# A 1-D max pool on one core: every load first, outputs kept on chip, stores queued behind the last load in longer runs

## The chip, the core and the metric

The kernel runs on one core of a Trainium2 chip. The metric is the device time in microseconds of one execution.

## The reference

The input is 32 x 256 rows of 4096 fp32 values. Each row is cut into 256 windows of 16 values, and the output is the maximum of each window.

```
x: (32, 256, 4096) float32, output_size = 256
for i in range(output_size):
    start = int(i * length / output_size)
    end = int((i + 1) * length / output_size)
    result[:, :, i] = np.max(x[:, :, start:end], axis=-1)
```

So 8192 rows of 16 KB come in (134.2 MB), and 8192 rows of 1 KB go out (8.4 MB). There is one comparison for each value. The work is moving bytes.

## The kernel before

Rows are dealt out in 7 groups of 9 rows for each of the 128 partitions, with one more row per partition at the end. A ring of nine 16 KB slots in SBUF, the memory on the chip, takes three loads of three rows. Each load reads a contiguous run of 48 KB per partition. VectorE reduces row by row into an output tile of the group. Two groups are stored while loads still run; five are "held" and stored behind the loads. Towards the end the loads get smaller (three, two, two, one, one rows, then quarters of a row), so that VectorE has little left to do when the last bytes arrive.

```python
    RING = 9
    G = 9
    N_GROUPS = 7
    LOAD = 3
    LATE = [3, 2, 2, 1, 1]
    HELD = 4
    PIECES = 4
    # ... ring, 6 output tiles, last_out; row = (g * 128 + p) * 9 + r
    for g in range(N_GROUPS):
        o = outs[g % len(outs)]
        sizes = LATE if g == N_GROUPS - 1 else [LOAD] * (G // LOAD)
        r = 0
        for n in sizes:
            at = n_read % RING
            nc.sync.dma_start(out=ring[:, at : at + n], in_=xg[g][:, r : r + n])
            for i in range(n):
                nc.vector.reduce_max(
                    out=o[:, (r + i) * O : (r + i + 1) * O],
                    in_=ring[:, at + i],
                    axis=mybir.AxisListType.X,
                )
            n_read += n
            r += n
        if g < N_GROUPS - 1 - HELD:
            nc.scalar.dma_start(out=og[g], in_=o)     # groups 0 and 1: among the loads
        else:
            held.append((og[g], o))
    # ... the last row, in PIECES pieces
    for dst, src in held:
        nc.sync.dma_start(out=dst, in_=src)           # five stores behind the loads
    nc.scalar.dma_start(out=ol, in_=last_out)
```

Of the kernel before, what the change touches and what calls it, by code (L numbers as in the profile page):

```python
# [1 line left out]

# [4 lines left out]


@with_exitstack
def kernel(  # L10
    ctx: ExitStack,
    tc: tile.TileContext,
    x: bass.AP,
    output_size: bass.AP,
    out: bass.AP,
):



    nc = tc.nc  # L20
    P = nc.NUM_PARTITIONS
    fp32 = mybir.dt.float32

    B, C, L = x.shape
    O = int(output_size)
    assert L % O == 0, (L, O)
    W = L // O
    xf = x.flatten_outer_dims()
    of = out.flatten_outer_dims()
    rows = xf.shape[0]  # L30
    assert rows == 64 * P

    RING = 9
    G = 9
    N_GROUPS = 7
    LOAD = 3
    LATE = [3, 2, 2, 1, 1]
    HELD = 4
    PIECES = 4

    pool = ctx.enter_context(tc.tile_pool(name="pool", bufs=1))
    ring = pool.tile([P, RING, O, W], fp32, tag="ring", name="ring")
    outs = [
        pool.tile([P, G * O], fp32, tag=f"out{i}", name=f"out{i}")
        for i in range(N_GROUPS - 1)
    ]
    last_out = pool.tile([P, O], fp32, tag="lastout", name="lastout")

    main = N_GROUPS * G * P
    xg = xf[0:main].rearrange("(g p r) (o w) -> g p r o w", p=P, r=G, w=W)  # L50
    og = of[0:main].rearrange("(g p r) m -> g p (r m)", p=P, r=G)
    xl = xf[main:rows].rearrange("p (o w) -> p o w", w=W)
    ol = of[main:rows]

    n_read = 0
    held = []
    for g in range(N_GROUPS):
        o = outs[g % len(outs)]
        sizes = LATE if g == N_GROUPS - 1 else [LOAD] * (G // LOAD)
        r = 0  # L60
        for n in sizes:
            at = n_read % RING
            nc.sync.dma_start(out=ring[:, at : at + n], in_=xg[g][:, r : r + n])
            for i in range(n):
                nc.vector.reduce_max(  # L65
                    out=o[:, (r + i) * O : (r + i + 1) * O],
                    in_=ring[:, at + i],
                    axis=mybir.AxisListType.X,
                )
            n_read += n  # L70
            r += n
        if g < N_GROUPS - 1 - HELD:
            nc.scalar.dma_start(out=og[g], in_=o)
        else:
            held.append((og[g], o))

    at = n_read % RING
    oc = O // PIECES
    for c in range(PIECES):
        cut = slice(c * oc, (c + 1) * oc)  # L80
        nc.sync.dma_start(out=ring[:, at, cut], in_=xl[:, cut])
        nc.vector.reduce_max(  # L82
            out=last_out[:, cut], in_=ring[:, at, cut], axis=mybir.AxisListType.X
        )

    for dst, src in held:
        nc.sync.dma_start(out=dst, in_=src)
    nc.scalar.dma_start(out=ol, in_=last_out)


# [1 line left out]
_INS = ['x', 'output_size']  # L92
_OUTS = [((32, 256, 256), 'float32')]

_NUMBERS = {'output_size': 256}


# [26 lines left out]
```

## Time and profile before

| | before |
|---|---|
| time, median of 3 runs | 336.75 us (336.65 to 336.76) |
| span in the profile | 334.8 us |
| bytes moved | 142.6 MB, mean 426 GB/s |
| VectorE busy | 278.8 us, 83% |
| first data packet starts / last ends | 1.74 / 333.63 us |

Lines of the page of the kernel before: the busy engines, the row of DMA share by slice (40 slices, in tenths, 9 is 90% or more), packets, the queue of instruction fetches (packets, MB, share of 16 engines), the chain that ended last, and the costliest group (busy us, mean ns of one, idle time before it).

```profile
span 334.8 us, 174 instructions
...
DVE 278.8 (83%) x67; POOL 0.2 (0%) x4
...
DMA  9899999999998999899998999989999999999997
...
DMA packets 5041, 142.62 MB, mean 426 GB/s; under 512 B 560, under 2 KB 688, under 8 KB 1200
...
q14 instruction: 1, 0.01, 0.0%
...
DMA 61%; DVE 34%; issue 2%; DVEq 0%
...
L65 DVE TENSOR_REDUCE out<-ring 128x256 f32<-128x4096 f32 x63 | 274.3, 4412 | 50.0 <-DMA ring<-in_x_dram 50.0
```

A packet is what one of the 16 DMA engines moves at a time; here it is one contiguous run, so a run of 48 KB is one packet. The DMA row is full from end to end; that is the limit. The chain (61% DMA, 34% DVE) must not be read as a division of the blame. It passes through reductions because a load has to wait for a ring slot. While it waits there, one other load is being moved and another is queued, so the engines that move data are not idle.

The windows view shows this in numbers. Its columns are the window, its length, the busy time of VectorE with its number of instructions, the same for GpSimd, the clock, the DMA share, and GB/s. A packet is counted where it starts and with its whole time, so a short window can come out a little above 1.00.

```profile
20.00:60.00 40.00, 37.01 (x9) 0.00 (x0) 1.00 1.00 433
60.00:80.00 20.00, 14.36 (x4) 0.00 (x0) 1.00 1.00 420
...
314.00:326.00 12.00, 12.00 (x5) 0.00 (x0) 1.00 1.02 424
...
331.00:335.00 4.00, 0.00 (x0) 0.00 (x0) 1.00 0.43 173
```

The rate is 433 GB/s while only loads run. The Trainium skill, "DMA: Bandwidth & Descriptors", section "Where 436 GB/s comes from", gives a ceiling of 435 GB/s for the 16 ports; this trace agrees. The same section adds that between HBM, the memory that holds input and output, and SBUF a lower limit of about 358 GB/s binds; here, with one core at work, it does not, and the measurement decides. At 433 GB/s the 142.6 MB take 329.4 us of the 334.8. Little more than 5 us could be gained by any rearrangement, and start and end need part of that.

Next, lines of the timeline of the kernel before (start us, duration us, engine, line, operation, output<-input, count, idle time before and its releaser): the reductions on both sides of the first store, and the tail.

```profile
61.38 13.07 DVE L65 TENSOR_REDUCE out<-ring 128x256 f32<-128x4096 f32 x3 [1.46 <-DMA ring<-in_x_dram]
78.72 13.07 DVE L65 TENSOR_REDUCE out<-ring 128x256 f32<-128x4096 f32 x3 [4.27 <-DMA ring<-in_x_dram]
...
285.24 39.03 DVE L65 TENSOR_REDUCE out<-ring 128x256 f32<-128x4096 f32 x9 [1.53 <-DMA ring<-in_x_dram]
...
294.88 29.75 SPq L87 DMA_DIRECT2D out_dram<-out  x5
324.19 4.59 DVE L82 TENSOR_REDUCE lastout<-ring 128x64 f32<-128x1024 f32 x4
328.81 0.34 ACTq L88 DMA_DIRECT2D out_dram<-lastout  x1
```

Reductions of one load take 13.07 us and normally start 14.53 us apart. After the store among the loads the step is 78.72 - 61.38 = 17.34 us: 2.8 us for the store. VectorE ends at 328.8, close to the end of the span.

### The profile page before, as it was taken

The numbers are of one execution on the slowest core, as the hardware profiler recorded it, in microseconds if no ns is written. First come the engines' busy times: TensorE is split into PE (matmuls) and PEld (weight loads), VectorE is DVE, ScalarE is ACT, GpSimd is POOL, SyncE is SP. The second block draws the span as 40 slices with busy tenths as digits, with TensorE's granted clock in tenths as the row PEclk, the third lists the DMA queues.
The fourth block names the chain that finished last, engine by engine and source line by source line (L and its number), as shares of the span: only waits on it lengthen the run. The fifth ranks groups of instructions, "written<-read, shape, count | busy, mean of one in ns | idle before, by whom it ended". The sixth has DMA issues, their size and how long they took to land.

```text
span 334.8 us, 174 instructions
## 1 busy us (share of the span) xinstructions
DVE 278.8 (83%) x67; POOL 0.2 (0%) x4
## 2 busy tenths in 40 slices
DVE  0088989885988959798988989898898988999992
POOL 0000000000000000000000000000000000000000
DMA  9899999999998999899998999989999999999997
GB/s 370 382 470 446 399 470 393 461 386 439 435 464 382 429 464 464 382 470 423 423 470 376 470 452 393 470 382 464 452 393 470 399 446 431 435 416 411 411 433 315
DMA packets 5041, 142.62 MB, mean 426 GB/s; under 512 B 560, under 2 KB 688, under 8 KB 1200
## 3 DMA queue, kind: packets, MB, share of 16 engines
q1 hardware_dynamic: 4608, 140.12, 97.4%
q10 hardware_dynamic: 432, 2.49, 1.8%
q14 instruction: 1, 0.01, 0.0%
HBM read 134.22 MB, written 8.39 MB: 426 GB/s over the span
## 4 chain that ended last, share of the span: by engine, by line
DMA 61%; DVE 34%; issue 2%; DVEq 0%
DMA ring<-in_x_dram 61%; DVE out L65 33%; DVE lastout L82 1%; DVEq L119 0%; DVEq L65 0%
## 5 line engine op out<-in xcount | busy, mean ns | idle before, releaser
L65 DVE TENSOR_REDUCE out<-ring 128x256 f32<-128x4096 f32 x63 | 274.3, 4412 | 50.0 <-DMA ring<-in_x_dram 50.0
L82 DVE TENSOR_REDUCE lastout<-ring 128x64 f32<-128x1024 f32 x4 | 4.6, 1208 | 0.0
L105 POOL MEMSET const-bfloat16-1.0<- 128x1 bf16 x1 | 0.1, 102 | 0.0
L105 POOL MEMSET const-uint8-127<- 128x1 uint8 x1 | 0.1, 102 | 0.0
L105 POOL MEMSET const-float32-0.0<- 128x1 f32 x1 | 0.1, 99 | 0.2 <-issue 0.2
L105 POOL MEMSET const-float32-1.0<- 128x1 f32 x1 | 0.1, 99 | 0.0
## 6 DMA issues: line engine op xcount, KB each, us to landing
ring<-in_x_dram SPq DMA_DIRECT2D x19, 6144.0 KB, 30.5
ring<-in_x_dram SPq DMA_DIRECT2D x2, 4096.0 KB, 30.0
out_dram<-out SPq DMA_DIRECT2D x5, 1152.0 KB, 14.8
ring<-in_x_dram SPq DMA_DIRECT2D x2, 2048.0 KB, 30.9
out_dram<-out ACTq DMA_DIRECT2D x2, 1152.0 KB, 21.5
ring<-in_x_dram SPq DMA_DIRECT2D x4, 512.0 KB, 27.8
out_dram<-lastout ACTq DMA_DIRECT2D x1, 128.0 KB, 5.2
```

Of the source, the lines that this page charges most:

```text
L65: nc.vector.reduce_max(out=o[:, (r + i) * O : (r + i + 1) * O], in_=ring[:, at + i], axis=mybir.AxisListType.X,)
L82: nc.vector.reduce_max(out=last_out[:, cut], in_=ring[:, at, cut], axis=mybir.AxisListType.X)
L105: nc = _bacc.Bacc("TRN2", target_bir_lowering=False, num_devices=1)
```

## The change

The change puts all loads first, in 48 KB runs to the end; keeps all outputs in SBUF; and queues all stores behind the last load, in runs of 21 KB for each partition instead of 9 KB. The groups become three of 21 rows. The small late loads go, and so does the tile for the last row: its result lands in a ring slot that is free by then.

```diff
-    G = 9
-    N_GROUPS = 7
+    G = 21
+    N_GROUPS = 3
     LOAD = 3
-    LATE = [3, 2, 2, 1, 1]
-    HELD = 4
-    PIECES = 4
+    CUT = 15
     ...
     for g in range(N_GROUPS):
-        o = outs[g % len(outs)]
-        sizes = LATE if g == N_GROUPS - 1 else [LOAD] * (G // LOAD)
-        ...
-        if g < N_GROUPS - 1 - HELD:
-            nc.scalar.dma_start(out=og[g], in_=o)
-        else:
-            held.append((og[g], o))
+        for r in range(0, G, LOAD):
+            at = n_read % RING
+            nc.sync.dma_start(
+                out=ring[:, at : at + LOAD], in_=xg[g][:, r : r + LOAD]
+            )
+            for i in range(LOAD):
+                pooled(outs[g][:, (r + i) * O : (r + i + 1) * O], ring[:, at + i])
+            n_read += LOAD
     ...
+    spare = ring[:, (at + LOAD) % RING].rearrange("p o w -> p (o w)")[:, 0:O]
+    nc.sync.dma_start(out=ring[:, at], in_=xl)
+    pooled(spare, ring[:, at])
+    for g in range(N_GROUPS - 1):
+        nc.sync.dma_start(out=og[g], in_=outs[g])
+    for a, b in ((0, CUT), (CUT, G)):
+        nc.sync.dma_start(
+            out=og[N_GROUPS - 1][:, a * O : b * O],
+            in_=outs[N_GROUPS - 1][:, a * O : b * O],
+        )
-    nc.scalar.dma_start(out=ol, in_=last_out)
+    nc.scalar.dma_start(out=ol, in_=spare)
```

More of the change, by code (lines that the diff above doesn't have):

```diff
@@ L44 @@
         pool.tile([P, G * O], fp32, tag=f"out{i}", name=f"out{i}")
-        for i in range(N_GROUPS - 1)
+        for i in range(N_GROUPS)
     ]
-    last_out = pool.tile([P, O], fp32, tag="lastout", name="lastout")
     main = N_GROUPS * G * P
@@ L53, with pooled @@
     ol = of[main:rows]
+    def pooled(dst, src):
+        nc.vector.reduce_max(out=dst, in_=src, axis=mybir.AxisListType.X)
     n_read = 0
-    held = []
     for g in range(N_GROUPS):
-        o = outs[g % len(outs)]
-        sizes = LATE if g == N_GROUPS - 1 else [LOAD] * (G // LOAD)
-        r = 0
-        for n in sizes:
+        for r in range(0, G, LOAD):
             at = n_read % RING
-            nc.sync.dma_start(out=ring[:, at : at + n], in_=xg[g][:, r : r + n])
-            for i in range(n):
-                nc.vector.reduce_max(
-                    out=o[:, (r + i) * O : (r + i + 1) * O],
-                    in_=ring[:, at + i],
-                    axis=mybir.AxisListType.X,
-                )
-            n_read += n
-            r += n
-        if g < N_GROUPS - 1 - HELD:
-            nc.scalar.dma_start(out=og[g], in_=o)
-        else:
-            held.append((og[g], o))
-    at = n_read % RING
-    oc = O // PIECES
-    for c in range(PIECES):
-        cut = slice(c * oc, (c + 1) * oc)
-        nc.sync.dma_start(out=ring[:, at, cut], in_=xl[:, cut])
-        nc.vector.reduce_max(
-            out=last_out[:, cut], in_=ring[:, at, cut], axis=mybir.AxisListType.X
-        )
-    for dst, src in held:
-        nc.sync.dma_start(out=dst, in_=src)
-    nc.scalar.dma_start(out=ol, in_=last_out)
+            nc.sync.dma_start(
[4 more added lines that the diff above has]
+            n_read += LOAD
+    at = n_read % RING
+    spare = ring[:, (at + LOAD) % RING].rearrange("p o w -> p (o w)")[:, 0:O]
[7 more added lines that the diff above has]
+            in_=outs[N_GROUPS - 1][:, a * O : b * O],
+        )
+    nc.scalar.dma_start(out=ol, in_=spare)
 _INS = ['x', 'output_size']
```

## The prediction

> **What bounds the kernel now: bytes through the 16 DMA engines.** The windows view gives a DMA share of 1.00 and 433 GB/s from 20 to 60 us and about 416 to 429 GB/s in the tail from 285 to 330 us. The Trainium skill, "DMA: Bandwidth & Descriptors", section "Where 436 GB/s comes from", states a ceiling of 435 GB/s; this trace agrees. All 142.6 MB at 433 GB/s would take 329.4 us of the 334.8 us span. VectorE is 83% busy; in the timeline it takes 13.07 us for a load that arrives every 14.53 us, so it waits for DMA (50.0 us in the wait view). The chain's 34% DVE misleads: a load waits there for a ring slot while two other loads keep the engines full.
>
> **Where the 334.8 us go** (packet records of the trace). First packet at 1.74 us. Then packet time, summed and divided by 16 engines: about 330.4 us at median packet times, plus 1.2 us of packets slower than the median (start-up packets; some at 60 to 75 us, where the first store mixes with loads). The engines run out between 332.5 and 333.6 us; the end follows 1.2 us later.
>
> **Bytes do not change:** 134.2 MB in, 8.4 MB out.
>
> **What it does to packets.** Medians: 48 KB 1815 ns, 32 KB 1216, 16 KB 615, 9 KB 347, 4 KB 161, 1 KB 46; a fit is 0.0366 ns per byte plus 9 to 15 ns per packet. Estimates from it: 21 KB 799, 15 KB 573, 6 KB 235 ns. New sum: 2688 x 1815 + 128 x (615 + 2 x 799 + 573 + 235 + 46) = 5.27 ms, over 16 = 329.5 us: 1.0 us less. About half comes from the loads (4 KB pieces and the 16 and 32 KB loads), half from the 21 KB stores. Not mixing stores 1 and 2 into the load stream saves an estimated 0.2 to 0.3 us more.
>
> **What it moves.** Two stores, about 2.7 us each, leave the middle (17.3 and 17.0 us between starts of reductions become 14.5), and come back as writes at the end: off the load path, but not off the DMA engines. So the last 48 KB load lands earlier, near 308 us, the last 16 KB load near 313, and VectorE ends near 326 instead of 328.8. The stores, 19 us, run from 313 to about 332. Each is queued before its turn (the fourth near 321, its turn near 330). The small last store, issued near 326, gets in between. Pure writes already run at full rate: 347 ns a packet from 320 to 333 us. So VectorE's longer last reduction (about 4.4 us against pieces of 1.2) is hidden.
>
> **Critical path:** DMA engines throughout, so only the saved packet time counts: 1.3 us of 336.75. Time 335.4 us; 8 in 10: 334.7 to 336.3. Faster by over 2%: 0.005; within 2%: 0.98; slower: 0.015.
>
> **Right if the profile shows:** DMA share 1.00 from 3 to 331 us; reductions every 14.5 us without the two longer gaps; 21 KB packets near 800 ns; VectorE ending 6 us before the last packet; first packet and end gap unchanged.
>
> **Wrong if:** the new row pitch (336 instead of 144 KB between partitions) makes 48 KB packets slower than 1815 ns; a 19 us burst of writes slows below 27 bytes per ns per engine; or a store's issue is held by a semaphore (eight DMAs in rotation) so that the engines run dry before the end.

## The result, and the profile after

| | before | after |
|---|---|---|
| time, median of 6 runs each | 336.70 us (336.60 to 336.76) | 336.06 us (335.97 to 336.26) |
| span in the profile | 334.8 us | 334.3 us |
| data packets for each DMA engine | 280 | 216 |
| data packet time, summed, over 16 engines | 331.58 us | 330.64 us |
| last data packet ends | 333.63 us | 332.96 us |

The ratio is 0.9982, with a 95% interval from 0.9969 to 0.9995. Ratios are the mean time of one kernel's fast runs over that of the other's of the same rounds, so not quite the ratio of the medians. The change is a gain of about 0.6 us, 0.2%.

The same lines of the page of the changed kernel, with all its DMA queues:

```profile
span 334.3 us, 157 instructions
...
DVE 278.8 (83%) x64; POOL 0.2 (0%) x4
...
DMA  9899999999999999999999999999999999999997
...
DMA packets 3889, 142.62 MB, mean 427 GB/s; under 512 B 432, under 2 KB 560, under 8 KB 688
...
q1 hardware_dynamic: 3744, 142.48, 98.9%
q10 hardware_dynamic: 144, 0.13, 0.1%
q14 instruction: 1, 0.01, 0.0%
...
DMA 68%; DVE 26%; DVEq 2%; SPq 0%; issue 0%
...
L53 DVE TENSOR_REDUCE out<-ring 128x256 f32<-128x4096 f32 x63 | 274.5, 4412 | 47.6 <-DMA ring<-in_x_dram 47.6
```

VectorE is busy for the same 278.8 us, and the same 142.62 MB move in fewer packets. The chain now says 68% and 26%. That shift of 7 to 8 points went with a change of 0.2% in time: another reason not to read the chain as a division of the blame.

The same windows of the changed kernel:

```profile
20.00:60.00 40.00, 37.10 (x9) 0.00 (x0) 1.00 1.00 433
60.00:80.00 20.00, 17.08 (x5) 0.00 (x0) 1.00 1.00 433
...
314.00:326.00 12.00, 12.00 (x3) 0.00 (x0) 1.00 1.00 429
...
331.00:335.00 4.00, 0.00 (x0) 0.00 (x0) 1.00 0.25 98
```

The stretch from 60 to 80 us, which held the first store, is now pure loading at 433 GB/s. At the other end, 314 to 326 us are now stores alone, at 429 GB/s: a long burst of writes runs at nearly the rate of the loads. The DMA engines stop earlier in the last window: 98 instead of 173 GB/s.

The timeline of the changed kernel, around the place where the first store was, and the tail:

```profile
62.01 13.07 DVE L53 TENSOR_REDUCE out<-ring 128x256 f32<-128x4096 f32 x3 [1.45 <-DMA ring<-in_x_dram]
76.55 13.07 DVE L53 TENSOR_REDUCE out<-ring 128x256 f32<-128x4096 f32 x3 [1.47 <-DMA ring<-in_x_dram]
...
284.82 0.90 SPq L72 DMA_DIRECT2D out_dram<-out  x2
293.09 29.40 SPq L74 DMA_DIRECT2D out_dram<-out  x2
...
322.05 4.41 DVE L53 TENSOR_REDUCE ring<-ring 128x256 f32<-128x4096 f32 x1
326.49 0.38 ACTq L78 DMA_DIRECT2D out_dram<-ring  x1
```

The 17.34 us step is gone (76.55 - 62.01 = 14.54). The stores are issued at 284.8, 285.3, 293.1 and 322.2 us (the line with "29.40" covers the last two), while loads keep the engines busy until about 313. VectorE ends at 326.46, 6.5 us before the end of the last packet. Nearly all that the prediction named as signs is there, and the time lies in its range; the DMA share is 0.96 from 3 to 20 us and 0.98 from 326 to 331 us in the windows view, and not 1.00. The size is off: 0.64 us gained instead of 1.3.

The packet records of the trace show the durations themselves (median ns; estimates from the prediction in the last column):

```
packet     before   after   predicted
48 KB      1815     1818    1815
21 KB      -        799     799
15 KB      -        573     573
9 KB       347      -       -
6 KB       -        234     235
1 KB       46       46      46
```

The estimates for single packets hold within 1 ns except the 48 KB one. It is 3 ns longer, and 168 of them an engine make 0.5 us of recorded time. The new row pitch (the distance in memory between the rows of two partitions) is not the reason. In the changed kernel the median is 1815 ns in the first five loads and 1818 to 1820 ns from the seventh on, and it is the same at the old pitch in the second run below, which has no store among the loads either. In the kernel before, the packets stay at 1815 ns until the eleventh load, past both of its stores among the loads, and rise only then; in a run below with seven stores among the loads they stay there until the fourteenth. Landings are 14.50 us apart with the short packets and 14.53 us with the long ones. Against the kernel before this costs the changed one about 0.2 us (up to 4 ns for each of 8 packets an engine, in loads 6 to 12). Why a store among the loads has this effect is open.

The question for the experiments is what the records are worth in time, and which part of the change brings the 0.6 us.

### The profile page after: what moved, and what is told of

Same layout as the page of the kernel before. It is cut to its first block, busy times and chain, and to the rows that moved or that the text cites. A ratio compares the mean times of both kernels' runs of the same rounds, so it can differ in the third digit from the quotient of the medians.

```text
span 334.3 us, 157 instructions
## 1 busy us (share of the span) xinstructions
DVE 278.8 (83%) x64; POOL 0.2 (0%) x4
## 2 busy tenths in 40 slices
DMA packets 3889, 142.62 MB, mean 427 GB/s; under 512 B 432, under 2 KB 560, under 8 KB 688
## 4 chain that ended last, share of the span: by engine, by line
DMA 68%; DVE 26%; DVEq 2%; SPq 0%; issue 0%
DMA ring<-in_x_dram 68%; DVE out L53 25%; DVEq L109 2%; DVE ring L53 1%; SPq L59 0%
## 5 line engine op out<-in xcount | busy, mean ns | idle before, releaser
L53 DVE TENSOR_REDUCE ring<-ring 128x256 f32<-128x4096 f32 x1 | 4.4, 4410 | 0.0
```

The costliest lines, as they stand in the source:

```text
L53: nc.vector.reduce_max(out=dst, in_=src, axis=mybir.AxisListType.X)
```

## Experiments

Theory A: the 16 DMA engines are the limit from end to end, and a packet costs less than its record says, because successive packets overlap a little (the records of one instant add up to 16.02 to 16.4 busy engines out of 16). Rival B: the gain comes from taking the stores out of the middle. Rival C: recorded packet time counts in full. Later a theory F joins: the slowest of the 16 engines sets the end.

### One part of the change at a time

The first four runs were made on one chip, beside each other. The first keeps the stores of before and takes the new load sizes.

```diff
-    LATE = [3, 2, 2, 1, 1]
-    PIECES = 4
+    LATE = [3, 3, 3]
+    PIECES = 1
```

> Only the load sizes change (all 48 KB runs to the end, last load in one 16 KB piece); the seven 9 KB-run stores stay as before. Theory A (the 16 DMA engines are the limit, but successive packets overlap by some 6 ns, so a packet's recorded time does not count in full): 40 fewer load packets per engine, about 0.25 us less, 336.45. Rival C (recorded packet time counts in full): 0.49 us less, 336.2. Rival B (the gain comes from getting stores out of the middle): unchanged, 336.7.

Measured: 336.90 us (336.77 to 337.03), ratio 1.0005 (0.9992 to 1.0017), against 336.72 for before. A and C expected a gain that did not come; the interval holds B's "unchanged", but the trace shows another reason than B's. The timeline of this run's tail shows why:

```profile
314.97 13.07 DVE L65 TENSOR_REDUCE out<-ring 128x256 f32<-128x4096 f32 x3 [1.83 <-DMA ring<-in_x_dram]
327.96 4.41 DVE L82 TENSOR_REDUCE lastout<-ring 128x256 f32<-128x4096 f32 x1
...
332.40 0.34 ACTq L88 DMA_DIRECT2D out_dram<-lastout  x1
```

With the two stores still among the loads, the last 48 KB load lands late, and VectorE then has 13.07 + 4.41 us of reductions to do. It ends at 332.4 instead of 328.8. By the packet records the last load lands 0.22 us earlier than before (319.30 instead of 319.52), so the fewer packets did help. The large stores end 0.30 us earlier (333.07 instead of 333.37), in part because the last small store no longer runs among them: it waits for VectorE and ends at 333.76 instead of 333.63. The small late loads of before were there to prevent just this. In the changed kernel they are not needed, because all stores lie behind the loads and hide VectorE's tail.

The second run moves only the two early stores to the end.

```diff
-    HELD = 4
+    HELD = 6
-        for i in range(N_GROUPS - 1)
+        for i in range(N_GROUPS)
-    last_out = pool.tile([P, O], fp32, tag="lastout", name="lastout")
+    last_out = ring[:, (at + LOAD) % RING].rearrange("p o w -> p (o w)")[:, 0:O]
```

> Only the position of the first two stores changes: all seven 9 KB-run stores go behind the last load; loads as before. A: only the mixing of reads and writes at two places goes, about 0.2 us: 336.5. B: the whole gain, 336.06. In the trace the two longer gaps between reductions (17.3 and 17.0 us) become 14.5.

Measured: 336.42 us (336.26 to 336.53), ratio 0.9990 (0.9978 to 1.0003). That is 0.30 us below before: near A's 0.2, half of what B needs. The interval holds both, so the time alone does not decide; all five runs lie above B's 336.06. The packet records show where it came from. Of the 48 KB packets that start between 58 and 80 us, 40 took over 1850 ns in the kernel before, 48 in the first run, and 3 here. The excess over 1816 ns of that stretch comes to 0.49 us for each engine in the kernel before, and 0.02 us here. Against it stand the 48 KB packets of loads 6 to 12, which are longer here by 0.18 us an engine in all, as told above. The difference, 0.29 us, is what the time shows.

The third run has the new stores (at the end, in 21 KB runs) and the old small late loads (LATE and PIECES of before, put into the changed kernel).

> Stores as in the changed kernel (all at the end, 21 KB runs), loads in the small late pieces of before. Against the run that only moves the stores: A 0.05 us less (336.45), C 0.2 us less. The rest to 336.06 is then the loads'.

Measured: 336.14 us (335.98 to 336.51), ratio 0.9983 (0.9971 to 0.9996): 0.28 us less than the run that only moves the stores.

The fourth is the changed kernel once more.

> The changed kernel once more, on the chip of the three others: 336.06 again, 0.64 us below before, if the result is not the chip's. In the trace: one 8 KB instruction fetch inside the span, which lengthens one packet of one DMA engine by about 0.66 us. If the slow first packet of one engine (3165 ns, and from there a landing spread of 1.25 us instead of 0.56) comes from the change, it is there again; if it is chance, it is not, or in another size.

Measured: 336.00 us (335.78 to 336.24), ratio 0.9977 (0.9964 to 0.9991). In its trace one engine again finishes its first packet late, 0.77 us after the others, and the landings of the first load are spread over 1.29 us. It is not a slow packet this time: it took 1813 ns but started at 3.54 us, where all the others had started by 2.31. More on that below.

On this chip the steps were therefore 336.72, then 336.42 with the stores moved, 336.14 with longer store runs as well, 336.00 with larger loads as well. Each step is of the size of the scatter between runs, so only their order of size should be taken from this. Load sizes alone, without the moved stores, gave nothing: the parts are not independent.

### What a packet costs

The next run makes the disputed cost large. The changed kernel stores its outputs in 1 KB runs. The rows land in permuted places: the result is wrong.

```diff
-    og = of[0:main].rearrange("(g p r) m -> g p (r m)", p=P, r=G)
+    og = of[0:main].rearrange("(g r p) m -> g p r m", p=P, r=G)
```

> The changed kernel with the 63 output rows of each partition stored in 1 KB runs (the rows land in permuted places, so the result is wrong on purpose). 504 packets an engine instead of 32 for the same bytes. Theory A (successive packets overlap by some 6 ns): 40 ns a packet, stores 20.2 us instead of 19.2, 337.0. Rival C (recorded 46 ns count in full): stores 23.2 us, 340.0. The loads land as in the changed kernel, the last 48 KB one at 309.

Measured: 338.52 us (338.42 to 338.67), ratio 1.0055 against before. The changed kernel had 0.9979 on the same chip in the next set of runs, so 472 more packets per engine cost (1.0055 - 0.9979) x 336.7 = 2.6 us: 5.4 ns each. The recorded durations say 8.4 ns each (504 x 46 ns against 19.2 us for the 32 longer packets). C's 340.0 is too high and A's 337.0 too low; the truth is between them. The overlap itself can be read from this trace: from 314 to 326 us, with 1 KB stores alone, the records add up to 17.38 busy engines out of 16, so a record of 46 ns overlaps the next one by 46 x (1 - 16/17.38) = 3.7 ns. Of the 8.4 ns, about 4.7 then count, near the measured 5.4. In the load phase of the changed kernel the same reckoning gives 3.5 ns a packet.

A milder form, with a right result, regroups the rows so that a store has 3 KB runs and a load is one contiguous block of 6 MB.

```diff
-    xg = xf[0:main].rearrange("(g p r) (o w) -> g p r o w", p=P, r=G, w=W)
-    og = of[0:main].rearrange("(g p r) m -> g p (r m)", p=P, r=G)
+    xg = xf[0:main].rearrange("(g a p r) (o w) -> g a p r o w", p=P, r=LOAD, a=G // LOAD, w=W)
+    og = of[0:main].rearrange("(g a p r) m -> g p a (r m)", p=P, r=LOAD, a=G // LOAD)
```

> The changed kernel with rows regrouped so that each load is one contiguous 6 MB block (still 48 KB runs, row pitch 48 instead of 336 KB) and each store is cut into 3 KB runs, all stores at the end; the result is right. 136 more packets an engine than the changed kernel. From the run with 1 KB runs (2.6 us for 472 more packets, 5.5 ns each): 0.75 us more than the changed kernel, 336.75; by recorded packet times 1.1 us more. If the row pitch mattered for the loads, they would no longer land every 14.53 us.

Measured: 336.85 us (336.79 to 336.88), 0.87 us above the changed kernel's 335.98 of the same set. That is 6.4 ns for each of the 136 extra packets. The loads still land every 14.53 us, so the row pitch (48 KB here, 336 KB in the changed kernel, 144 KB before) does not matter once they run. The Trainium skill, "DMA: Bandwidth & Descriptors", section "Latency and other measured facts", warns of large powers of two as row pitch; none of these is one, and no run here shows such a loss.

The same page, section "Why small descriptors are slow (HBM only)", gives about 3 cycles of fixed overhead for a packet and 32 bytes of descriptor metadata. With 27 bytes per ns and engine as measured, and if those cycles are of the 850 MHz that the page has for the fabric (it does not say so), that is an estimate of 4.7 ns. The measured 5.4 to 6.4 ns agree in order of size, while the 9 to 15 ns of the prediction's fit are two to three times as much.

### Stores among the loads

The next run stores the first group's output in seven pieces of 384 KB among the loads, each as soon as it is ready, in the 3 KB layout.

```diff
             n_read += LOAD
+            if g == 0:
+                nc.scalar.dma_start(
+                    out=og[g][:, r // LOAD], in_=outs[g][:, r * O : (r + LOAD) * O]
+                )
...
-    for g in range(N_GROUPS - 1):
+    for g in range(1, N_GROUPS - 1):
```

> The same, but the first group's output (2.75 MB) is stored in 7 pieces of 384 KB in the middle of the loads, as each is ready; 14 pieces' worth stays at the end, which leaves enough stores to hide VectorE's tail. Against the run with all at the end: 1.05 us more if every interruption of the loads costs 0.15 us (two such stores cost 0.30 us in the run that only moved them), 0.35 us more if the cost goes with the bytes that are mixed in, nothing if that 0.30 us was scatter.

Measured: 337.50 us (337.41 to 337.79), 0.65 us above the run with all at the end. But the windows view of its tail shows that this is no cost of mixing:

```profile
332.00:334.00 2.00, 1.19 (x1) 0.00 (x0) 1.00 0.18 71
334.00:336.00 2.00, 0.00 (x0) 0.00 (x0) 1.00 0.19 66
```

Between 332 and 334 us the engines are nearly idle (a share of 0.18). VectorE ends at 333.2 here, the stores left at the end are too short to hide it, and the last small store comes late, as in the first run. The run was badly designed for its question, and none of its three expectations is tested by the time. The landings do answer part of it. The eighteenth load lands 6.52 us later than in the run with all at the end (270.79 against 264.27, first engine each). Seven such pieces take 7/21 of the 20.07 us between the last load's landing and that of the last large store at the end, less 0.37 us for the small store that runs within it: 6.57 us. So on balance these seven stores cost the loads nothing beyond their bytes and packets. The balance hides two effects: in loads 6 to 14 the 48 KB packets stay near 1815 ns here instead of 1819 (0.29 us less for each engine), so the interruptions themselves can have cost some 0.2 us, of which at most 13 slow load packets are 0.07. The slow packets of the kernel before belong to the first of its two 9 KB stores alone; the second (104 to 125 us) has none. Why that first store disturbed 40 load packets is open.

### Is VectorE hidden, and with how much to spare?

This run drops the stores of the first two groups (a wrong result; 5.5 MB less to move).

```diff
-    for g in range(N_GROUPS - 1):
-        nc.sync.dma_start(out=og[g], in_=outs[g])
```

> The changed kernel without the stores of the first two groups (5.5 MB less, result wrong on purpose). If VectorE's last reductions, which end at 326.5 us, are hidden under the stores with some 6 us to spare and nothing else, the time falls by about 4.7 us to 331.3 and not by the 12.8 us that the bytes are worth (which would be 323.2). If the chain through VectorE (25% of the page's chain) already bounded the kernel, it would not fall.

Measured: 330.78 us (330.70 to 330.88), ratio 0.9825. It fell by 5.2 us (from 336.0) and not by the 12.8 us that the bytes are worth. The windows of its tail:

```profile
312.00:316.00 4.00, 4.00 (x2) 0.00 (x0) 1.00 1.01 431
316.00:326.00 10.00, 10.00 (x3) 0.00 (x0) 1.00 0.27 111
326.00:329.00 3.00, 0.35 (x1) 0.00 (x0) 1.00 0.13 44
```

From 316 to 326 us the DMA share is 0.27 while VectorE is busy for all 10.00 us. So VectorE's tail is the next limit, about 5 us below the DMA's. In the changed kernel it is hidden with that much to spare. This confirms the prediction's step about the last reduction, and refutes a reading of the chain by which VectorE bounds the kernel.

### The slowest engine, and the fetch inside the span

Every trace with 64 or more reductions has one 8 KB instruction fetch in the middle of the span (the "q14 instruction: 1" of both pages). It takes about 325 ns on one DMA engine, and one data packet of that engine then takes 0.66 us longer (2478 instead of 1818 ns in the changed kernel, 1875 instead of 1216 in the kernel before). From there to the end that engine lags. Fewer instructions should do away with it: one reduction for each load instead of three.

```diff
-            for i in range(LOAD):
-                pooled(outs[g][:, (r + i) * O : (r + i + 1) * O], ring[:, at + i])
+            pooled(
+                outs[g][:, r * O : (r + LOAD) * O],
+                ring[:, at : at + LOAD].rearrange("p r o w -> p (r o) w"),
+            )
```

> The changed kernel with one reduction instruction for each load instead of three (22 instead of 64). The loads that VectorE reads, the bytes and the DMAs are the same. Theory F (the end is set by the slowest DMA engine, and the 8 KB instruction fetch inside the span holds one engine back by 0.66 us): with fewer instructions the fetch goes, and the last packets end closer together; 0.1 to 0.6 us less than the changed kernel's 336.0, depending on whether a slow start-up packet holds another engine back as far. Rival (the fetch hides in slack): the same 336.0.

Measured: 335.68 us (335.55 to 336.08), ratio 0.9972 (0.9960 to 0.9985). The DMA queues of its page:

```profile
q1 hardware_dynamic: 3744, 142.48, 99.0%
q10 hardware_dynamic: 144, 0.13, 0.1%
```

There is no third queue any more: the fetch is gone. The same was done to the kernel before (one reduction for each load).

> The kernel before with one reduction for each load. F: the fetch goes and the time falls by about 0.5 us, to 336.2; rival: 336.7 as before. No other part of the change is in it.

Measured: 336.26 us (335.99 to 336.34), ratio 0.9986 (0.9973 to 1.0000): about 0.4 us less than before. In the kernel before, the fetch's engine landed last, 1.21 us after the first engine in the last large store; here that spread is 0.81 us. The changed kernel and its fused form were then run side by side.

> The changed kernel unchanged, for a direct comparison with the next run and the two above: 336.0, with one instruction fetch inside the span.

> The changed kernel with one reduction for each load, again, beside the changed kernel itself: no fetch in the span, 0.3 us less than the changed kernel (335.7) if the fetch's engine ended last; if the earlier difference was the chip's or chance, the same.

Measured: 335.98 us (335.87 to 336.05), ratio 0.9979, and 335.86 us (335.47 to 336.00), ratio 0.9974. The 0.12 us between the medians are within the scatter. The traces tell why so little was gained here. In the changed kernel one engine is already 1.0 us behind after the first load (1.03 us between the first and the last landing, 0.67 us behind the last but one), because its first packet took long (3165 ns in the first trace) or started late (at 3.09 us here). The fetch puts another engine as far behind, so removing it leaves the first where it is (1.15 us in the fused run). Such a lag also eats into the gain of the change: chained engine by engine, the last packets end 0.8 us earlier on the mean of the 16 engines than in the kernel before (332.0 on average of the three traces, against 332.8), but the slowest engine, which sets the time, only 0.65 us.

```
landings of the first load, first to last engine, us, by row pitch of the loads
144 KB: before 0.56, loads only 0.77, stores moved 0.67, before fused 0.76
336 KB: changed kernel 1.28, 1.29, 1.03; fused 0.87, 1.15; old late loads 1.04; 1 KB runs 0.80; two dropped 1.05
 48 KB: 3 KB runs 1.11, with seven stores among the loads 1.07
```

All four traces at 144 KB are below all ten at other pitches. That is a hint that the address layout decides how unevenly the engines start, and no more: no experiment changed the pitch alone.

The fused form of the changed kernel was the fastest right version in both sets that had it, 335.68 and 335.86 us. It is 0.3% below the kernel before, and not surely below the changed kernel.

## Why the prediction was right, and where its sum was off

- **"What bounds the kernel now: bytes through the 16 DMA engines"**: right. The bytes did not change, and neither did the time, within 0.2%. In a sense the whole prediction is this: at 433 GB/s the bytes take 329.4 us, and no order of the transfers shortens that.
- **"So VectorE's longer last reduction ... is hidden"**: right. It ends at 326.5 us against a last packet at 333.0, and the run without two stores shows some 5 us to spare. The prediction did not say that this holds only with all stores at the end. The load sizes alone were no gain (336.90 against 336.72), because there VectorE's tail was exposed.
- **"Pure writes already run at full rate"**: nearly. 314 to 326 us run at 429 GB/s, against 433 for loads.
- **"New sum: ... 1.0 us less"**: this is the term that was mis-sized. Longer runs in loads and stores together measured 0.42 us (336.42 with the stores only moved, 336.00 with all). Two errors add up. First, the sum of before contained the 4-byte completion packets (16 at the end of each DMA), and the new one left out its own (432 of them at 9 ns, over 16 engines: 0.24 us). Like for like the sums differ by 0.74 us, or 11.6 ns for each of the 64 data packets saved per engine (8 completion packets go with them). Second, the measured worth of a packet is 5.4 to 6.4 ns, and the records show why it is less: successive packets overlap by about 3.5 ns. With that, 64 packets are 0.35 to 0.41 us. The measured 0.42 agrees, but only within the scatter of some 0.1 us, and the lag of the slowest engine is in it too.
- **"About half comes from the loads ..., half from the 21 KB stores"**: not shown by its own numbers (by these the stores give 0.18 us), and not by the runs: 0.28 us for the stores and 0.14 for the loads, each with a scatter of about 0.1. Their split stays open.
- **"Not mixing stores 1 and 2 into the load stream saves an estimated 0.2 to 0.3 us more"**: right in size, 0.30 us, but by luck: 0.49 us of slow packets went, more than estimated, and 0.18 us of longer 48 KB packets came. The slow packets came from the first store alone, and seven smaller stores among the loads cost nothing on balance, so it is no rule about mixing.
- **"first packet and end gap unchanged"**: nearly. The first packet starts at 1.73 instead of 1.74 us, and the gap from the last packet to the end of the span is 1.30 instead of 1.16 us.
- **The three dangers named**: two did not come. The burst of writes kept its rate, and the four large stores were issued 7 us or more before their turn. The first came in part: 48 KB packets went from a median of 1815 ns to 1818, though not through the row pitch, since the run that only moves the stores has the old pitch and the same longer packets. It is a term that the sum had wrong by some 0.2 us.

## What to carry to other kernels

When the DMA engines are full from the first microsecond to the last, first divide the bytes by the measured rate: the distance from that to the span is all that reordering can win. A packet's worth should be taken from a run with many more packets and not from recorded durations, which overlap. Small late loads and stores queued behind the loads are two cures for the same exposed tail, so judge such parts together: here larger loads were no gain as long as two stores stayed among the loads.

## What the Trainium skill lacked or had wrong

- "DMA: Bandwidth & Descriptors" gives no figure for how far recorded packet times overlap (3.5 to 3.7 ns here): a fit of the records gave 9 to 15 ns of fixed time per packet, while extra packets cost 5.4 ns (472 of them) and 6.4 ns (136).
- "Runtime: NRT & Kernel Launch" has instruction fetches in the middle of a run, but no page says what one costs the transfers beside it: here 8 KB and 325 ns lengthened one data packet by 0.66 us and left that engine among the last. With one reduction per load (115 instead of 157 instructions in the profile) it was gone.
- "DMA: Bandwidth & Descriptors" tells nothing of the uneven start: first packets of 48 KB took up to 3199 ns instead of 1818 or started up to 1.8 us after the first one, and the landings of the first load were spread over 0.56 to 1.29 us; most of that lag stays until the end.
- The same page, section "Issuing engines are not separate DMA queues", says that transfers interleave, and names no cost. Here the first store among the loads made 40 load packets slow (0.49 us of packet time per engine), the second none, and seven smaller ones at most 13 (0.07 us).
- No page that was consulted tells of the slow rise of a read packet's time: 48 KB took 1815 ns in the first five loads and 1818 to 1820 from about the seventh on, but from the twelfth with two stores among the loads, and from the fifteenth with seven.
